# Hybrid attention and RG-LRU layer: x loaded ahead of the modulation weights, an early 64-byte read, and the scaling of x moved behind the first h

## The chip, the cores and the metric

The kernel runs on one core of one Trainium2 chip. A core has TensorE (PE, with its weight loads as PEld), VectorE (DVE), ScalarE (ACT), GpSimd (POOL) and SyncE (SP), which work side by side and wait for each other through semaphores, and 16 DMA engines that serve the transfers issued from SP and ACT. The metric is the device time of one execution in microseconds, as the median of several runs.

## The reference, cut to what matters

The input x is 512 rows of 1024 float32. Everything in the opening serves the modulated, normalised h and its first product:

```python
c_act = jax.nn.silu(c)
mod = c_act @ w_mod[l] + b_mod[l]
shift, scale, gate = jnp.split(mod, 3, axis=-1)
h = rmsnorm(x, norm_gain[l]) * (1.0 + scale[:, None, :]) + shift[:, None, :]
proj = h @ w_in[l]
```

The 3072 columns of proj feed block-sparse causal attention (8 heads of 64, rotary), a gated linear recurrence with a width-4 convolution, and two SiLU gates. Both branches are normalised and gated, go through one output projection, and are added to x with the gate; a last RMSNorm follows.

## The kernel before, in words

All products run on TensorE in a split form: each operand is a high part (rounded to TensorE's fp32r) and a low part (what is left), and three products of parts stand for one float32 product. h is kept transposed, as eight chunks h0 to h7 of 128 channels by 512 rows. The first phase makes h chunk by chunk and multiplies each with the first seven column blocks of w_in (`w0_d`, 896 columns): 21 matmuls of 512 columns a chunk (L406), which accumulate in seven PSUM banks (`acc`). The remaining blocks follow, with attention, recurrence and gates woven in, then the output projection (`po`).

What one chunk d needs:

- **x**: four row tiles x0 to x3 (128 rows by 1024). ACT squares and sums each (L334, `scr`), takes the root (L338, `ss`), DVE takes the reciprocal (L340). Then the tile is scaled by its row factor in place (L344 on ACT or L346 on DVE, columns 128 to 1023). Columns 0 to 127, which chunk 0 needs, are scaled apart into `xs`. TensorE transposes the four tiles' columns of a chunk into a PSUM bank `xp` (L392 for chunk 0, L388 for the others).
- **g**: two columns, gain and shift of the chunk. DVE multiplies the chunk's modulation weights (`ws`, from the array `wss`, one row of shift and one of scale for each channel) by the broadcast SiLU of c (`cb`) and sums along the row (L368 for chunk 0, in four halves of 512; L372 for the rest, two of 1024). Three small operations make g of the sums (L376, L377, L380).
- **h**: ACT applies g to `xp` twice (L395), once rounded (`h0h`), once not; DVE's subtraction (L397) gives the low part `h0l`.
- **w0**: ACT rounds the weights (L231, `w00512h` and `w00384h` in chunk 0), DVE subtracts (L249, `w00512l`).

All transfers of the opening are issued by SP in program order on one queue. Until h0 is there, TensorE is given 42 matmuls on a constant tile (`warm`, L306), whose result nobody reads.

The order of the instructions is set at build time by a planner (`Plan.emit`): every `op` has an engine, an estimated cost, the buffers that it reads and writes, an earliest start (`after`) and a due time. The planner walks through an estimated time and gives each engine the ready operation with the earliest due time; an operation with a second way (`alt`) may go to either engine. Changing a due time or a cost can so reorder engines far behind the place of the edit. Each engine then runs its list strictly in that order.

Of the kernel before, what the change touches and what calls it, by code (L numbers as in the profile page):

```python
# [10 lines left out]
AF = mybir.ActivationFunctionType  # L11
OP = mybir.AluOpType
# [3 lines left out]
D = 1024  # L16
# [3 lines left out]
BIG = 3.0e38  # L20
LRU_C = 8.0
NFIRST = 7
NWARM = 42
MOVE = 3.4

V_GAIN, V_SHIFT, V_SCALE, V_GATE = 0, 8, 16, 24
# [33 lines left out]
class Plan:  # L60
# [11 lines left out]
    def op(self, eng, cost, fn, r=(), w=(), due=None, table=None, lat=0.25, after=0.0, alt=None):  # L72
        o = Op(eng, cost, fn, list(r), list(w), due, table, lat, after, alt)
        deps = set()
        for b in o.r:
            if b.writer is not None:
                deps.add(b.writer)
        for b in o.w:
            if b.writer is not None:
                deps.add(b.writer)  # L80
            deps.update(b.readers)
        for b in o.r:
            b.readers.append(o)
        for b in o.w:
            b.writer, b.readers = o, []
        for b in set(o.r) | set(o.w):
            b.users += 1
        deps.discard(o)
        o.deps = list(deps)
        for d in deps:  # L90
            d.outs.append(o)
        o.left = len(deps)
        self.ops.append(o)
        return o
# [82 lines left out]
def tile_hymba_block(ctx: ExitStack, tc: tile.TileContext, x, wss, wgt, win0, wv, winr,  # L177
                     wo, wg, vecs, fgain, consts, out):
    nc = tc.nc
    V, A, G, PE, SP = nc.vector, nc.scalar, nc.gpsimd, nc.tensor, nc.sync  # L180
# [18 lines left out]
    op = plan.op  # L199
# [4 lines left out]
    def t4(name, dt=F32, shape=(128, 1024)):  # L204
        return Buf("t4", list(shape), dt, name)

    def bank(name, kind=None):
        return Buf("ps", [128, 512], F32, name, kind)

    def col(name):  # L210
        return Buf("c", [128, 2], F32, name)

    def fix(name, shape, dt=F32):
        return Buf("fix", list(shape), dt, name)


    def dv(n, ptr=0):
        return 0.075 + n / 960.0 + 0.06 * ptr

    def dv2(n, ptr=0):  # L220
        return 0.14 + n / 1920.0 + 0.06 * ptr

    def ac(n, ptr=0, acc=0):
        return 0.09 + n / 1200.0 + 0.1 * ptr + 0.1 * acc

    def acp(n, ptr=0, acc=0):
        return ac(n, ptr, acc) - 0.039
# [6 lines left out]
    def pe(n, passes=1):  # L234
        return passes * n / 2250.0

    def load(dst, src, due, kb=512, queue=SP):
        op("SP", kb / 390.0, lambda: queue.dma_start(dst[:], src), [], [dst], due, lat=1.1 if due < T_REST - 8 else 3.3)  # L238
# [17 lines left out]
    def like(t):  # L256
        return lambda name, dt: t4(name, dt, t.shape)


    def t_first(d):  # L260
        return T_FIRST + 4.79 * d

    T_FIRST, T_REST, STEP = 12.3, 50.7, 0.94

    def t_step(n):
        return T_REST + STEP * n
# [3 lines left out]

    xt = [t4(f"x{t}") for t in range(NT)]
    vec, ident, cst = fix("vec", [128, NV]), fix("ident", [128, 128]), fix("cst", [128, 2048])
    load(vec, vecs, -100, kb=40)
    for t in range(NT):
        load(xt[t], x[t * 128:(t + 1) * 128, :], -99 + 0.5 * t)
    ws, w0 = {}, {}
    for d in range(ND):
        if d == 0:
# [25 lines left out]
    op("V", 0.3, lambda: V.memset(warm[:], 1.0), [], [warm], -10)  # L304
    for n in range(NWARM):
        op("PE", 0.32 if n < 11 else 0.235, lambda: PE.matmul(spare[:], warm[:, 0:128], warm[:], start=True, stop=True),  # L306
# [9 lines left out]
    cb = t4("cb")  # L316
# [10 lines left out]


    xs = [Buf("t2", [128, 128], F32, f"xs{t}") for t in range(NT)]
    xdue = (5.0, 6.3, 7.6, 8.9)  # L330
    scr = [t4("scr0"), t4("scr1")]
    for t in range(NT):
        ss, due = col("ss"), xdue[t]
        op("A", ac(1024, 0, 1), lambda t=t, ss=ss: A.activation(  # L334
            scr[t % 2][:], xt[t][:], AF.Square, accum_out=ss[:, 0:1]), [xt[t]], [scr[t % 2], ss], due,
           alt=("V", dv(1024), lambda t=t, ss=ss: V.scalar_tensor_tensor(
               scr[t % 2][:], xt[t][:], 1.0, xt[t][:], op0=OP.mult, op1=OP.mult, accum_out=ss[:, 0:1])) if t == 9 else None)
        op("A", 0.2, lambda ss=ss: A.activation(ss[:, 1:2], ss[:, 0:1], AF.Sqrt, bias=epsc[:, 0:1], scale=1.0 / D),  # L338
           [ss, epsc], [ss], due + 0.2, "sqrt")
        op("V", 0.1, lambda ss=ss: V.reciprocal(ss[:, 0:1], ss[:, 1:2]), [ss], [ss], due + 0.3)  # L340
        for dst, cut, late in ((xs[t], slice(0, 128), 0.4), (xt[t], slice(128, D), 2.5)):
            o = (lambda d_, c_: d_[:] if d_ in xs else d_[:, c_])
            n = cut.stop - cut.start
            op("A", ac(n, 1), lambda t=t, ss=ss, dst=dst, cut=cut, o=o: A.activation(  # L344
                o(dst, cut), xt[t][:, cut], AF.Copy, scale=ss[:, 0:1]), [ss, xt[t]], [dst], due + late,
               alt=("V", dv2(n, 1), lambda t=t, ss=ss, dst=dst, cut=cut, o=o: V.tensor_scalar(  # L346
                   o(dst, cut), xt[t][:, cut], ss[:, 0:1], None, op0=OP.mult)))


    h = [t2(f"h{d}") for d in range(ND)]  # L350
# [4 lines left out]
                                         op0=OP.add), [vec], [vec], -3)  # L355

    sch = col("sch")

    def part(d, j):
        return ws[d][j][:, j] if d >= 4 else ws[d][j][:]  # L360

    def gain(d):

        sc, g = col("sc"), col("g")
        for j in (1, 0):
            if d == 0:
                for n in range(2):
                    op("V", dv(512), lambda j=j, n=n: V.scalar_tensor_tensor(  # L368
                        ws[0][j][n][:], ws[0][j][n][:], 1.0, cb[:, 512 * n:512 * n + 512], op0=OP.mult, op1=OP.mult,
                        accum_out=(sch if n else sc)[:, j:j + 1]), [ws[0][j][n], cb], [ws[0][j][n], sch if n else sc], 7 + n)  # L370
                continue
            op("V", dv(1024), lambda j=j: V.scalar_tensor_tensor(  # L372
                part(d, j), part(d, j), 1.0, cb[:], op0=OP.mult, op1=OP.mult, accum_out=sc[:, j:j + 1]),
               [ws[d][j], cb], [ws[d][j], sc])
        if d == 0:
            op("V", 0.1, lambda: V.tensor_add(sc[:], sc[:], sch[:]), [sc, sch], [sc], 10)  # L376
        op("V", 0.2, lambda: V.tensor_scalar(  # L377
            g[:, 1:2], sc[:, 1:2], vec[:, V_SCALE + d:V_SCALE + d + 1], vec[:, V_GAIN + d:V_GAIN + d + 1],
            op0=OP.add, op1=OP.mult), [sc, vec], [g])
        op("V", 0.1, lambda: V.tensor_add(g[:, 0:1], sc[:, 0:1], vec[:, V_SHIFT + d:V_SHIFT + d + 1]), [sc, vec], [g])  # L380
        return g

    for d in range(ND):
        g, xp = gain(d), bank(f"xp{d}")

        def turn(xp=xp, d=d):
            for t in range(NT):
                PE.transpose(xp[:, t * 128:(t + 1) * 128], xt[t][:, d * 128:(d + 1) * 128], ident[:])  # L388
        if d:
            op("PE", 0.44, turn, xt + [ident], [xp], t_first(d) - 3.8)  # L390
        for t in range(NT if not d else 0):
            op("PE", 0.11, lambda t=t, xp=xp: PE.transpose(xp[:, t * 128:(t + 1) * 128], xs[t][:], ident[:]),  # L392
               [xs[t], ident], [xp], 7 + 0.5 * t)
        for o in (hh[d], h[d]):
            op("A", acp(512, 2), lambda o=o, d=d, xp=xp, g=g: A.activation(  # L395
                o[:], xp[:], AF.Identity, bias=g[:, 0:1], scale=g[:, 1:2]), [xp, g], [o])
        op("V", dv(512), lambda d=d: V.tensor_sub(hl[d][:], h[d][:], hh[d][:].bitcast(F32)), [h[d], hh[d]], [hl[d]])  # L397
        if d:
            wp = [split(w0[d], like(w0[d]), f"w0{d}", 128 * NFIRST)] * 2
        else:  # L400
            wp = [split(w, lambda name, dt, w=w: Buf("t2", w.shape, dt, name), w.name, w.shape[1], late=[g]) for w in w0[0]]
        for i, (a, b) in enumerate(((0, hh[d]), (1, hh[d]), (0, hl[d]))):
            for j in range(NFIRST):
                w, k = wp[j // 4][a], j if d else j % 4
                op("PE", pe(512), lambda w=w, k=k, b=b, j=j, first=(d == 0 and i == 0), last=(d == ND - 1 and i == 2):
                   PE.matmul(acc[j][:], w[:, k * 128:(k + 1) * 128], b[:], start=first, stop=last),  # L406
                   [w, b], [acc[j]], t_first(d) + (0.62 if d else 1.6) * i + 0.21 * j)
# [329 lines left out]
    for g in range(4):  # L737
        br, half = "la"[g // 2], g % 2
# [11 lines left out]
        for t in range(NT):  # L750
            m = slice(t * 128, (t + 1) * 128)
            cuts = (0, 256, 512) if g == 3 and t == NT - 1 else (0, 512)
            for n, (lo, up) in enumerate(zip(cuts, cuts[1:])):
# [15 lines left out]
                o, q = t2("o"), half + n  # L769
                if w < 512:  # L770
                    op("V", dv(w, 1), lambda t=t, c0=c0, c1=c1, o=o, q=q: V.scalar_tensor_tensor(
                        o[:, :c1 - c0], res[t][:, c0:c1], 1.0, res[t][:, c0:c1], op0=OP.mult, op1=OP.mult,
                        accum_out=ssq[t][:, q:q + 1]), [res[t]], [ssq[t], o], t1 + 0.2)
# [107 lines left out]
```

## Time and profile before

| What | Value |
|---|---|
| Median of 3 runs | 243.88 us (243.81 to 247.26) |
| The profiled execution's own time | 243.72 us |
| Its span, first to last instruction | 242.0 us |
| PE busy | 232.3 us (96%) |
| DVE busy | 196.2 us (81%) |
| ACT busy | 144.3 us (60%) |
| Mean granted TensorE clock | 0.994 |

The profile and the trace are of one execution. Times inside it are counted from the start of its span; the 1.72 us between span and execution time lie outside of all instructions. Busy times of consecutive instructions overlap by their pipelines, so a matmul of 0.39 us can follow the one before after 0.23 us; where a sum is made, the distance from start to start counts.

### The profile page before, as it was taken

How to read it: one execution, taken by the hardware profiler on the slowest of the kernel's cores; microseconds unless marked ns; L12 is line 12 of the kernel's file. 1: busy time of each engine (PE TensorE's matmuls, PEld its weight loads, DVE VectorE, ACT ScalarE, POOL GpSimd, SP SyncE). 2: the span in 40 equal slices, each digit the busy share in tenths (PEclk: the TensorE clock that was granted, in tenths of full speed). 3: DMA queues.
4: the chain of work that ended last, by engine and by line, in shares of the span. 5: the costliest groups of instructions: out<-in, count | busy, mean ns of one | idle time of the engine just before them, and what ended most of it. 6: DMA issues, size and time to landing. Idle time of an engine off the chain costs nothing.

```text
span 242.0 us, 3301 instructions
## 1 busy us (share of the span) xinstructions
PE 232.3 (96%) x1134; PEld 184.5 (76%) x1134; DVE 196.2 (81%) x364; ACT 144.3 (60%) x264; POOL 12.0 (5%) x32
## 2 busy tenths in 40 slices
PE   7899999999999989999999999999999999999990
PEld 4357888888888868788888688886888868888880
DVE  3499989979745899996799999999999999326473
ACT  7685373675224296439899999695664934003362
POOL 1000000018800000000000000000000000000000
PEclk9999999999999999999999999999999999999997
DMA  6999999922799877045079997292221300000045
GB/s 211 311 408 409 419 417 412 368 91 57 171 270 230 209 282 227 37 173 173 0 178 297 208 270 265 77 364 83 88 88 39 134 3 0 0 0 0 3 160 186
DMA packets 15087, 44.29 MB, mean 183 GB/s; under 512 B 2144, under 2 KB 2784, under 8 KB 14432
## 3 DMA queue, kind: packets, MB, share of 16 engines
q1 hardware_dynamic: 14928, 43.96, 54.9%
q8 instruction: 9, 0.15, 0.3%
q10 hardware_dynamic: 144, 0.13, 0.2%
q14 instruction: 6, 0.05, 0.1%
HBM read 35.69 MB, written 2.10 MB: 156 GB/s over the span
## 4 chain that ended last, share of the span: by engine, by line
PE 78%; DMA 9%; ACT 4%; SPq 3%; DVE 2%; issue 1%; ACTq 0%
PE acc L406 16%; PE pj L241 10%; PE pj L243 9%; PE pj L242 9%; PE po L241 6%; PE po L243 6%; PE po L242 6%; DMA wc<-in_winr_dram 6%; PE av L582 4%; PE sc L559 4%; DMA x<-in_x_dram 3%; PE tp L603 3%; SPq L465 2%; ACT x L344 1%; SPq L238 1%; PE xp L388 1%
## 5 line engine op out<-in xcount | busy, mean ns | idle before, releaser
L570 ACT ACTIVATE z<-z,mn 128x128 f32<-128x128 f32 (+3 forms) x32 | 17.8, 557 | 10.8 <-DVE mn L567 10.6
L567 DVE CUSTOM_DVE_ANT_0 z<-sc,cst 128x128 f32<-128x128 f32 (+3 forms) x32 | 14.6, 485 | 6.2 <-PE sc L559 6.2
L372 DVE SCALAR_TENSOR_TENSOR ws<-ws,cb 128x1024 f32<-128x1024 f32 x14 | 16.8, 1219 | 0.0
L231 ACT COPY pt<-tp 128x128 f32<-128x128 f32 (+3 forms) x29 | 10.7, 415 | 9.4 <-PE tp L603 9.2
L306 PE MATMUL spare<-warm 128*128 128x512 bf16 x42 | 12.4, 435 | 1.5 <-DVE warm L304 1.5
L603 PE MATMUL tp<-ident,z 128*128 128x128 f32 x80 | 12.1, 273 | 0.6 <-ACT z L570 0.6
L603 PEld LDWEIGHTS tp<-ident,z 128*128 128x128 f32 x80 | 9.8, 140 | 3.6 <-ACT z L570 1.3
L775 ACT ACTIVATE o<-xr 128x512 f32<-128x512 f32 x7 | 4.4, 633 | 11.8 <-DVE xr L764 11.8
L764 DVE SCALAR_TENSOR_TENSOR xr<-po,rba,xr 128x512 f32<-128x512 f32 (+1 forms) x9 | 6.2, 691 | 6.3 <-PE po L243 6.2
L764 DVE SCALAR_TENSOR_TENSOR xr<-po,rbl,xr 128x512 f32<-128x512 f32 x8 | 6.0, 748 | 6.0 <-PE po L243 6.0
L530 DVE SCALAR_TENSOR_TENSOR wgt<-wgt,cb 128x1024 f32<-128x1024 f32 x8 | 9.8, 1219 | 0.0
L306 PEld LDWEIGHTS <-warm 128*128 128x128 bf16 x42 | 4.7, 113 | 6.6 <-issue 2.5
L747 DVE TENSOR_TENSOR wo<-wo,grow 128x1024 f32<-128x1024 f32 x8 | 9.7, 1214 | 0.0
L582 PE MATMUL av<-pt,v 128*64 128x512 f32 (+3 forms) x64 | 9.5, 439 | 0.0
L484 DVE SCALAR_TENSOR_TENSOR xc<-xl,vec,xc 128x511 f32<-128x511 f32 (+2 forms) x12 | 8.9, 743 | 0.1
L582 PEld LDWEIGHTS av<-pt,v 128*64 128x64 f32 x64 | 4.2, 136 | 5.2 <-issue 4.2
L625 ACT ACTIVATE sz<-pj 128x512 f32<-128x512 f32 x8 | 4.8, 597 | 3.7 <-PE pj L243 3.7
L729 ACT ACTIVATE rba<-ss,epsc 128x4 f32<-128x4 f32 x1 | 0.3, 263 | 10.2 <-PE ss L727 10.2
L626 DVE SCALAR_TENSOR_TENSOR sz<-sz,pj 128x512 f32<-128x512 f32 x8 | 5.5, 682 | 0.9 <-ACT sz L625 0.9
L395 ACT ACTIVATE h<-xp,g 128x512 f32<-128x512 f32 x8 | 6.2, 770 | 0.0
L570 ACT ACTIVATION_READ_ACCUMULATOR z<-z,mn 128x1 f32 x32 | 6.0, 188 | 0.0
L334 ACT ACTIVATE scr<-x 128x1024 f32<-128x1024 f32 x4 | 4.2, 1057 | 2.9 <-DMA x<-in_x_dram 2.9
(1119 smaller groups left out, 771.0 us busy)
## 6 DMA issues: line engine op xcount, KB each, us to landing
wc<-in_winr_dram SPq DMA_DIRECT2D x13, 512.0 KB, 5.4
ws<-in_wss_dram SPq DMA_DIRECT2D x4, 1024.0 KB, 12.8
wgt<-in_wgt_dram SPq DMA_DIRECT2D x8, 512.0 KB, 4.0
wo<-in_wo_dram SPq DMA_DIRECT2D x8, 512.0 KB, 4.1
w<-in_win_dram SPq DMA_DIRECT2D x7, 448.0 KB, 8.6
ws<-in_wss_dram SPq DMA_DIRECT2D x6, 512.0 KB, 7.9
x<-in_x_dram SPq DMA_DIRECT2D x4, 512.0 KB, 5.1
wv<-in_wv_dram SPq DMA_DIRECT2D x4, 512.0 KB, 7.6
```

The source lines that it names most:

```text
L231: op("A", acp(n) if psum else ac(n), lambda: A.copy(dst(), src()), r, w, due, after=after, alt=("V", dv(n) if psum else dv2(n), lambda: V. ...
L241: PE.matmul(ps, lh, rh, start=start, stop=False)
L242: PE.matmul(ps, lh, rl, start=False, stop=False)
L243: PE.matmul(ps, ll, rh, start=False, stop=stop)
L306: op("PE", 0.32 if n < 11 else 0.235, lambda: PE.matmul(spare[:], warm[:, 0:128], warm[:], start=True, stop=True), [warm], [spare], 5.3 + ...
L372: op("V", dv(1024), lambda j=j: V.scalar_tensor_tensor(part(d, j), part(d, j), 1.0, cb[:], op0=OP.mult, op1=OP.mult, accum_out=sc[:, j:j + ...
L406: PE.matmul(acc[j][:], w[:, k * 128:(k + 1) * 128], b[:], start=first, stop=last),
L567: op("V", dv(n) + 0.085, lambda s=s, z=z: V.tensor_tensor_reduce(out=z[:, :n], in0=ps[s][:, :n], in1=cst[:, 2048 - n:2048], op0=OP.add, op ...
L570: op("A", ac(n, 1, 1), lambda s=s, z=z: A.activation(z[:, :n], z[:, :n], AF.Exp, bias=mn[s][:, 0:1], scale=-1.0, accum_out=sm[:, i, s:s + ...
L582: PE.matmul(ps2[64 * s:64 * s + 64, k * 128:], vt[k][:, (2 * p + s) * 64:(2 * p + s + 1) * 64], pts[s][:, k, k * 128:], start=(k == 0), st ...
L603: PE.transpose(tp[:, k * 128:(k + 1) * 128], z[:, k * 128:(k + 1) * 128], ident[:])
L764: op("V", dv(w, 1), lambda t=t, ps=ps, c0=c0, c1=c1, br=br: V.scalar_tensor_tensor(res[t][:, c0:c1], ps[:, :c1 - c0], rb[br][:, t:t + 1], ...
```

## The change

It edits the opening. SP issues all four tiles of x before the modulation weights. ACT issues, as its first instruction, a transfer of 16 columns of the weights of chunk 0 (64 bytes on each of 128 rows) into a tile `touch` that nobody reads. The engines of the scaling are fixed: `xs0` and `xs1` on DVE, `xs2` and `xs3` and all four large scalings on ACT; those of x1, x2 and x3 are kept until after h0 by an earliest start (`REST`). The gain of chunk 0 is made of half sums with b_mod added in between, so that one small operation instead of three stands behind the last sum. The transposes of chunk 1 are due 2.2 us later, the constant matmuls are 31 instead of 42, and two base times of the planner are 0.5 us earlier.

```diff
-NWARM = 42
+NWARM = 31
+REST = (0.0, 12.9, 13.0, 13.1)
...
-    T_FIRST, T_REST, STEP = 12.3, 50.7, 0.94
+    T_FIRST, T_REST, STEP = 11.8, 50.2, 0.94
...
+    touch = fix("touch", [128, 16])
+    op("A", 0.1, lambda: A.dma_start(touch[:], wss[0][:, 0, 0:16]), [], [touch], -100)
     load(vec, vecs, -100, kb=40)
     for t in range(NT):
-        load(xt[t], x[t * 128:(t + 1) * 128, :], -99 + 0.5 * t)
+        load(xt[t], x[t * 128:(t + 1) * 128, :], -99 + 0.3 * t)
...
-    xdue = (5.0, 6.3, 7.6, 8.9)
+    xdue = (4.0, 5.0, 6.0, 7.0)
...
-        for dst, cut, late in ((xs[t], slice(0, 128), 0.4), (xt[t], slice(128, D), 2.5)):
+        for dst, cut, e, due2, after in ((xs[t], slice(0, 128), "VVAA"[t], due + 0.4, 0.0), (xt[t], slice(128, D), "A", 20.0 + t, REST[t])):
             o = (lambda d_, c_: d_[:] if d_ in xs else d_[:, c_])
             n = cut.stop - cut.start
-            op("A", ac(n, 1), lambda t=t, ss=ss, dst=dst, cut=cut, o=o: A.activation(
-                o(dst, cut), xt[t][:, cut], AF.Copy, scale=ss[:, 0:1]), [ss, xt[t]], [dst], due + late,
-               alt=("V", dv2(n, 1), lambda t=t, ss=ss, dst=dst, cut=cut, o=o: V.tensor_scalar(
-                   o(dst, cut), xt[t][:, cut], ss[:, 0:1], None, op0=OP.mult)))
+            if e == "A":
+                op("A", ac(n, 1), lambda t=t, ss=ss, dst=dst, cut=cut, o=o: A.activation(
+                    o(dst, cut), xt[t][:, cut], AF.Copy, scale=ss[:, 0:1]), [ss, xt[t]], [dst], due2, after=after)
+            else:
+                op("V", dv2(n, 1), lambda t=t, ss=ss, dst=dst, cut=cut, o=o: V.tensor_scalar(
+                    o(dst, cut), xt[t][:, cut], ss[:, 0:1], None, op0=OP.mult), [ss, xt[t]], [dst], due2, after=after)
...
+        half = (sc, sch)
         for j in (1, 0):
             if d == 0:
                 for n in range(2):
...
-                        accum_out=(sch if n else sc)[:, j:j + 1]), [ws[0][j][n], cb], [ws[0][j][n], sch if n else sc], 7 + n)
+                        accum_out=half[n][:, j:j + 1]), [ws[0][j][n], cb], [ws[0][j][n], half[n]], 8 - 2 * j + 0.7 * n)
+                    if not n:
+                        op("V", 0.1, lambda j=j, v=(V_SHIFT, V_SCALE)[j]: V.tensor_add(
+                            sc[:, j:j + 1], sc[:, j:j + 1], vec[:, v:v + 1]), [sc, vec], [sc], 9.2)
+                if j:
+                    op("V", 0.2, lambda: V.tensor_scalar(g[:, 1:2], sch[:, 1:2], sc[:, 1:2], vec[:, V_GAIN:V_GAIN + 1],
+                                                         op0=OP.add, op1=OP.mult), [sc, sch, vec], [g], 9.4)
+                else:
+                    op("V", 0.1, lambda: V.tensor_add(g[:, 0:1], sch[:, 0:1], sc[:, 0:1]), [sc, sch], [g], 9.5)
                 continue
...
         if d == 0:
-            op("V", 0.1, lambda: V.tensor_add(sc[:], sc[:], sch[:]), [sc, sch], [sc], 10)
+            return g
...
-            op("PE", 0.44, turn, xt + [ident], [xp], t_first(d) - 3.8)
+            op("PE", 0.44, turn, xt + [ident], [xp], t_first(d) - (3.8 if d > 1 else 1.6))
```

What that does to the order of the instructions is seen at three places. In the names, the number behind the underscore is a build number: x_90, x_99, x_116 and x_133 are the row tiles x0 to x3 before, x_92, x_101, x_118 and x_131 after, and ws_129 or ws_142 is the first half row of modulation weights.

SP's queue at the start, first before, then changed:

```order
L238 DMA x_116<-in_x_dram 128x1024
L238 DMA ws_129<-in_wss_dram 128x512
L238 DMA x_133<-in_x_dram 128x1024
L238 DMA ws_148<-in_wss_dram 128x512
L238 DMA ws_158<-in_wss_dram 128x512
```

```order
L239 DMA x_118<-in_x_dram 128x1024
L239 DMA x_131<-in_x_dram 128x1024
L239 DMA ws_142<-in_wss_dram 128x512
L239 DMA ws_148<-in_wss_dram 128x512
L239 DMA ws_159<-in_wss_dram 128x512
```

The fourth tile of x and the first half row of weights have changed places; all that follows on the queue is in the old order up to the fifties of microseconds.

ACT between the last squares and h, before and changed:

```order
L334 ACTIVATE scr_125,ss<-x_133 128x1024
L338 ACTIVATE ss<-ss,epsc 128x1
L344 ACTIVATE x_99<-x_99,ss 128x896
L344 ACTIVATE x_116<-x_116,ss 128x896
L231 CAST w00512h<-w_176 128x512
L344 ACTIVATE x_133<-x_133,ss 128x896
L395 ACTIVATE h0h<-xp_150,g 128x512
L395 ACTIVATE h_233<-xp_150,g 128x512
L231 CAST w01h<-w_1_224 128x896
L395 ACTIVATE h1h<-xp_226,g 128x512
```

```order
L337 ACTIVATE scr_127,ss<-x_131 128x1024
L341 ACTIVATE ss<-ss,epsc 128x1 x2
L348 ACTIVATE x_92<-x_92,ss 128x896
L348 ACTIVATE xs_190<-x_118,ss 128x128
L348 ACTIVATE xs_197<-x_131,ss 128x128
L232 CAST w00512h<-w_178 128x512
L232 CAST w00384h<-w_185 128x384
L409 ACTIVATE h0h<-xp_150,g 128x512
L409 ACTIVATE h_218<-xp_150,g 128x512
L348 ACTIVATE x_101<-x_101,ss 128x896
L348 ACTIVATE x_118<-x_118,ss 128x896
L348 ACTIVATE x_131<-x_131,ss 128x896
```

Ahead of `h0h`, three large scalings have become one, and two small ones and one more rounding have come in. The other three large ones stand between the second h of chunk 0 and `h1h`, and the rounding of `w01` has gone to DVE. On DVE the same stretch now reads:

```order
L374 SCALAR_TENSOR_TENSOR ws_142,sc<-ws_142,cb 128x512
L374 SCALAR_TENSOR_TENSOR ws_148,sch<-ws_148,cb 128x512
L343 RECIPROCAL ss<-ss 128x1 x2
L378 TENSOR_TENSOR sc<-sc,vec 128x1
L381 TENSOR_SCALAR g<-sch,sc,vec 128x1
L374 SCALAR_TENSOR_TENSOR ws_159,sc<-ws_159,cb 128x512
L374 SCALAR_TENSOR_TENSOR ws_167,sch<-ws_167,cb 128x512
L378 TENSOR_TENSOR sc<-sc,vec 128x1
L384 TENSOR_TENSOR g<-sch,sc 128x1
L250 TENSOR_TENSOR w00512l<-w_178,w00512h 128x512
L250 TENSOR_TENSOR w00384l<-w_185,w00384h 128x384
```

The four weighted sums stand close together; the two reciprocals that ACT's small scalings wait for are behind the second of them.

TensorE around the first matmuls with h, before and changed:

```order
L388 MATMUL xp_226<-ident,x_90 128x128
L388 MATMUL xp_226<-ident,x_99 128x128
L388 MATMUL xp_226<-ident,x_116 128x128
L388 MATMUL xp_226<-ident,x_133 128x128
L306 LDWEIGHTS warm
L306 MATMUL spare<-warm 128x512
L406 MATMUL acc_236<-h0h,w00512h 128x512
```

```order
L420 MATMUL acc_241<-h0h,w00384l 128x512
L420 MATMUL acc_222<-h0l,w00512h 128x512
L402 MATMUL xp_260<-ident,x_92 128x128
L402 MATMUL xp_260<-ident,x_101 128x128
L402 MATMUL xp_260<-ident,x_118 128x128
L402 MATMUL xp_260<-ident,x_131 128x128
L420 MATMUL acc_226<-h0l,w00512h 128x512
```

The transposes of chunk 1 stood ahead of chunk 0's first matmul and now stand behind its fifteenth. Eight constant matmuls stood between the transposes of `xs3` and those of chunk 1; now one stands behind `xs3`, and the two that stood within chunk 0's 21 matmuls are gone.

## Rows read from the trace of the kernel before

**Rows 1.** page, part 1: busy us, share of the span, instructions, by engine

```profile
PE 232.3 (96%) x1134; PEld 184.5 (76%) x1134; DVE 196.2 (81%) x364; ACT 144.3 (60%) x264; POOL 12.0 (5%) x32
```

**Rows 2.** chain of waits to 30 us: start us, us, engine, what, line

```profile
3.11 8.01 DMA x<-in_x_dram
...
11.14 1.16 ACT scr L334 x2
...
12.62 1.86 ACT x L344 x2
...
14.90 1.04 ACT x L344
15.94 0.68 ACT h0h L395
...
16.65 2.60 PE acc L406 x10
...
24.30 4.82 PE acc L406 x21
```

**Rows 3.** all waits of TensorE: who waited for whom, us, times, longest

```profile
PE spare L306 <- DVE warm L304: 1.5, 1, 1.5
PE xp L392 <- DVE xs L346: 1.1, 1, 1.1
PE tp L603 <- ACT z L570: 0.6, 1, 0.6
```

**Rows 4.** by stretches: PE, PEld, DVE, ACT, POOL busy; PEclk, DMA share, GB/s

```profile
4.00:5.00 1.00, 1.00 (x7) 1.00 (x6) 0.26 (x1) 0.50 (x3) 0.00 (x0) 1.00 1.01 397
7.00:9.00 2.00, 2.00 (x11) 1.03 (x10) 0.45 (x2) 1.60 (x6) 0.00 (x0) 1.00 0.97 157
12.00:13.00 1.00, 1.00 (x7) 0.49 (x5) 1.00 (x3) 0.97 (x4) 0.00 (x0) 1.00 1.04 396
```

**Rows 5.** ACT in order of time: start us, us, operation, idle before and releaser

```profile
4.77 1.06 ACT L334 ACTIVATE scr<-x 128x1024 f32<-128x1024 f32 x1 [0.49 <-DMA x<-in_x_dram]
...
6.17 1.06 ACT L334 ACTIVATE scr<-x 128x1024 f32<-128x1024 f32 x1 [0.25 <-DMA x<-in_x_dram]
...
7.91 1.06 ACT L334 ACTIVATE scr<-x 128x1024 f32<-128x1024 f32 x1 [0.40 <-DMA x<-in_x_dram]
...
8.96 0.47 ACT L338 ACTIVATE ss<-ss,epsc 128x1 f32<-128x1 f32 x2
...
14.39 0.60 ACT L231 CAST w00512h<-w 128x512 fp32r<-128x512 f32 x1
```

**Rows 6.** DVE in order of time, the same columns, around the sums

```profile
9.71 0.69 DVE L368 SCALAR_TENSOR_TENSOR ws<-ws,cb 128x512 f32<-128x512 f32 x1 [1.69 <-DMA ws<-in_wss_dram]
...
10.33 0.68 DVE L346 TENSOR_SCALAR x<-x,ss 128x896 f32<-128x896 f32 x1
...
11.82 0.69 DVE L368 SCALAR_TENSOR_TENSOR ws<-ws,cb 128x512 f32<-128x512 f32 x1
...
14.24 0.16 DVE L376 TENSOR_TENSOR sc<-sc,sch 128x2 f32<-128x2 f32 x1
...
16.94 1.23 DVE L372 SCALAR_TENSOR_TENSOR ws<-ws,cb 128x1024 f32<-128x1024 f32 x1
...
18.56 0.69 DVE L397 TENSOR_TENSOR h0l<-h,h0h 128x512 fp32r<-128x512 f32 x1
```

**Rows 7.** PEld in order of time: the constant matmuls' weight loads

```profile
5.78 0.15 PEld L306 LDWEIGHTS <-warm 128*128 128x128 bf16 x1 [0.28 <-issue]
6.21 0.15 PEld L306 LDWEIGHTS <-warm 128*128 128x128 bf16 x1 [0.28 <-issue]
...
7.06 1.22 PEld L306 LDWEIGHTS <-warm 128*128 128x128 bf16 x6 [0.28 <-issue]
```

**Rows 8.** groups by line and shape: xcount, busy us, mean ns of one

```profile
L231 ACT COPY pt<-tp 128x128 f32<-128x128 f32 x8 | 1.7, 265 | 3.3 <-PE tp L603 3.3
```

**Rows 9.** DMA issues of 5.2 to 5.5 us: KB, us to landing

```profile
w<-in_win_dram SPq DMA_DIRECT2D x1, 256.0 KB, 8.6
```

## The prediction, made before the changed kernel ran

> **What bounds the kernel now.** Read the busy shares first: TensorE is busy for 232.3 of 242.0 us [rows 1]. Its waits say the same more sharply: it waited three times in all, 1.5 us at the very start, 1.1 us for a scaled tile of x before h, and 0.6 us once in the middle [rows 3]. So the end of the kernel is set by when real matmuls begin, and by nothing that adds a wait behind that. The chain of waits then shows what sets the beginning [rows 2]: a transfer of x until 11.1, ACT's square and root of the last tile, large scalings of x at 12.62 and 14.90, h0h at 15.94, and the first matmul with h at 16.65. From there the chain is TensorE alone, 21 matmuls in 4.82 us, 0.23 each. The reader should see two costs in it: the last tile of x is late, and ACT does three large scalings that chunk 0 doesn't need before it makes h0h.
>
> Why is x late? ACT began the squares of x0, x1 and x2 when they landed, at 4.77, 6.17 and 7.91 [rows 5]; the fourth came only at 11.14. Half a row tile of weights was in between, which at 396 GB/s is 0.66 us. The rest is a hole: from 7 to 9 us the 16 DMA engines were as occupied as ever (share 0.97) but moved 157 GB/s instead of 397 [rows 4], so 480 KB are missing, or 1.2 us. Check: 7.91 + 1.40 (one tile, from x0 to x1) + 0.66 + 1.2 = 11.17. The hole falls on the first transfer that reads the modulation weights, the one that DVE waited for until 9.71 [rows 6]; the rate is back at 396 later, when the same array and w_in are read.
>
> **The change, part by part.** *x first.* The fourth tile should land at 7.91 + 1.40 = 9.31 in place of 11.14.
>
> *The early read.* No row shows one. Its cost lies between nothing (64 bytes a row, while the queues start up) and the whole hole of 1.2 us moved in front of x; its gain between nothing and the hole. I take that the hole goes: the slow stretch goes with a first access, and the first access is then made while vec and x start. The weights' halves then land at 9.97, 10.63, 11.3 and 11.95, and w0 of chunk 0, issued at about 5.3 and landed 8.6 later [rows 9], at about 12.6 and 13.1. ACT issues it ahead of its first work; x0 finds ACT idle for 0.49 us [rows 5], which covers an issue.
>
> *ACT to h0h.* Square 1.16 [rows 2] to 10.47; two roots 0.47 [rows 5] to 10.94; one large scaling, 0.93 (half of 1.86 [rows 2]), to 11.87; two 128-wide scalings at 0.27 each, by the 128-wide copy [rows 8], to 12.4; the 512-wide rounding when its weights land, 12.6, from start to next start 0.51 [rows 2, 5], to 13.1; the 384-wide one between 0.27 and 0.60, taken as 0.45, to 13.55.
>
> *DVE to g.* Four sums of 0.69, two reciprocals and four small operations of about 0.2 [rows 6]: 9.97 + 1.38 = 11.35, + 0.8 = 12.15, + 1.38 = 13.53, + 0.4 = 13.93. So DVE is the later by 0.4, and h0h starts at 13.95. Its 0.76 and the hand-over were 0.8 from ACT's start to the first matmul (0.68 and 0.71 after the overlap, by the chain [rows 2]): the first matmul at **14.75, 1.9 us earlier**.
>
> *Behind h0h.* Three large scalings, 0.93 each, stand after the second h, so the last tile is ready at 13.95 + 2 x 0.68 + 3 x 0.93 = 18.1. TensorE asks for it after fifteen matmuls: ten in 2.60 and five of 0.23 [rows 2] give 18.5. Not late, by 0.4. The low part h0l is closer: DVE does two subtractions (0.69, and 0.52 for 384 columns), two sums of 1.23 and h0l, 0.69 [rows 6], so 13.93 + 4.36 = 18.3; TensorE asks for it after fourteen matmuls, at 18.27. Then chunk 1: g needs 0.4 and one rounding of 896 columns, which is new on DVE (0.68, as x0's scaling [rows 6]), so h1h starts at 19.4 and feeds a matmul at 20.2; TensorE is through its four transposes and six matmuls at 18.5 + 0.44 + 1.38 = 20.3. Margins of 0 to 0.4 us, so I charge 0.2.
>
> *Work that changes on TensorE.* Chunk 1's transposes, 0.44, come into the stream; two constant matmuls, 0.46, leave it. Nothing.
>
> *Downstream.* DVE, ACT and TensorE are ordered a little differently from some 50 us on, because the planner starts from other times. I charge nothing: TensorE's real matmuls keep their order to the eighth column block, and its one wait there is 0.6.
>
> The sum against the profiled execution: 243.72 - 1.9 + 0.2 = 242.0. The median of the runs is 0.16 above that execution, so **242.1 us**, 0.7% faster.
>
> **A rule that bears on it.** The hole shows the DMA engines occupied and slow at once [rows 4]: what waits there waits on an engine, not in the queue. The Trainium skill ("DMA: Bandwidth & Descriptors", section "Issuing engines are not separate DMA queues") says that transfers issued from ACT and from SP end up on the same 16 engines and interleave. By that rule the slow first accesses of the early read are interleaved with x0 and hold it up; the sum would be that of the next paragraph, and no row here shows two queues at work in the opening.
>
> **The rivals.** *The hole stays, with the weights or in front of x.* Either way the weights land as before: x3 now ahead of them, the first half at 11.17, the second at 11.84. DVE goes 11.17 + 1.38 + 0.8 + 1.38 + 0.4 = 15.13, the first matmul at 15.95, a gain of 0.7 in place of 1.9, with the same 0.2 behind it: 243.88 - 0.5 = 243.4. For it: a slow first access has to be paid somewhere, and if the engines stand still for it, x pays. Against it: the read is issued before any tile of x is under way.
>
> *The clock falls (the slower side).* Before, TensorE had something to do until 16.65, its longest pause being 1.1 us, and the matmuls kept their pace. Eleven constant matmuls are taken out, those closest to h0. After the transposes of the last small tile, at 12.4, one is left: TensorE stands idle from about 12.7 to 14.75, 2.0 us. If that is enough, the first h matmuls run at the low level. At the start of the trace the constant matmuls follow at 0.43 us, 1.2 GHz for 512 columns, until 7.06, and at 0.20 to 0.23 then, the 2.4 GHz level [rows 7] (the granted clock reads 1.00 in all of these rows, so the spacing has to be read). That was 5.5 us from the first matmul at 1.5 [rows 3]. Another 5.5 us at 0.43 hold 12.8 matmuls that would take 2.95 us: a loss of 2.55, and 242.1 + 2.55 = 244.7, slower than before. It decides from a pause somewhere above the 1.1 us seen to be harmless. The Trainium skill ("TensorE: Matmul & The Clock Gate", section "Why this matters for your kernels") asks for no long pauses between bursts of matmuls, since the array then falls back to half its clock. Whether 2 us are long, no row here shows.
>
> *A new wait downstream.* DVE and ACT have other orders in the attention and gates; one more wait like the one seen costs 0.6 [rows 3], two 1.2: 242.7 to 243.3. For it: DVE is busy 81% of the whole span [rows 1]. Against it: TensorE waited once in all that time.
>
> **How the numbers follow.** The forecast has 0.47; the hole that stays 0.28; a new wait 0.13; the clock 0.09; 0.03 is left for more gain than I count, where roots, scalings and sums overlap better (241.0 and less). The predicted time is that of the likeliest, 242.1. The range reaches from 241.0, where ACT's and DVE's steps are all at the lower bounds, to 243.7, the hole that stays with a further 0.3 of waiting in chunks 0 and 1; it leaves out the clock case and the last 0.03. All of these lie within 2% of 243.88 (239.0 to 248.8), and 2% is about what a measurement of this kernel tells from no change: within 0.97, faster 0.01, slower 0.02, the last for a clock that falls and several new waits together.
>
> **What would show it.** In the profile after: the four squares of x without a pause, the last at about 9.3; no stretch before 14 us in which the DMA share is near 1 and the rate far below 390 GB/s; h0h at about 14 with DVE's g just before it; the first acc matmul at 14.75; a list of TensorE's waits with one of about 2 us before it and small ones in chunk 0 and 1; a spacing of 0.23 right after the pause. If the rate falls before x0 has landed, or again around 10 us, the hole stayed. If the spacing is 0.43 behind the pause, the clock fell. If the first matmul is 1.9 us earlier and the end is not, look for a new wait between 60 and 200 us: that would make the step "downstream: nothing" the wrong one.

## Result: 0.5% faster, within what counts as no change, and the profile after

The changed kernel ran in 242.79 us (median of 20 runs, 241.07 to 245.41) against 243.88 for the kernel before (20 runs); the ratio is 0.9946, interval 0.9926 to 0.9966. The ratios here and below leave out the executions more than 1.5% above the fastest of their kernel, three of these 20; the medians hold them. Forecast were 242.1 and "within 2%". A second series of 12 runs, the experiment *again* below, gave 243.18 and 0.9953 [0.9923, 0.9984]. What strikes is the spread: the executions of one kernel lie 4 us apart, and the fastest are 1.7 us better than the median. The profiled execution took 243.68 us, almost as long as the profiled one before.

TensorE's busy time (page, part 1; us, share, instructions) fell from 232.3 [rows 1], by its eleven constant matmuls fewer, and the span didn't follow (241.9, from 242.0):

```profile
PE 229.6 (95%) x1123; PEld 183.0 (76%) x1123; DVE 198.4 (82%) x367; ACT 142.5 (59%) x262; POOL 11.6 (5%) x32
```

So it stands still for longer. Read first where it starts with h. The chain of waits of the changed kernel (start us, us, what, line) answers to [rows 2]:

```profile
5.33 8.50 DMA w<-in_win_dram
...
13.85 0.62 ACT w00512h L232
...
14.79 0.78 ACT h0h L409
...
15.61 3.71 PE acc L420 x15
19.32 0.44 PE xp L402 x4
```

The first matmul with h stands at 15.61 in place of 16.65: 1.04 us earlier, not the 1.9 forecast. The chain no longer goes through x and its scalings; it goes through the transfer of chunk 0's w, which lands at 13.83. Why that is late, the stretches show (as in [rows 4]; us, PE, PEld, DVE, ACT and POOL busy, clock, DMA share, GB/s):

```profile
7.00:8.00 1.00, 1.00 (x6) 0.46 (x5) 0.04 (x1) 0.93 (x3) 0.00 (x0) 1.00 1.01 401
8.00:9.00 1.00, 1.00 (x6) 0.45 (x5) 0.41 (x2) 0.81 (x1) 0.00 (x0) 1.00 1.06 281
9.00:10.00 1.00, 0.91 (x5) 0.20 (x2) 0.41 (x2) 1.00 (x4) 0.00 (x0) 1.00 0.90 137
10.00:11.00 1.00, 0.90 (x5) 0.53 (x6) 0.26 (x2) 1.00 (x5) 0.00 (x0) 1.00 1.04 350
```

Engines occupied, 281 and 137 GB/s: the hole has stayed, behind x now. Against 400 GB/s, 8 to 11 us lack 119 + 263 + 50 = 432 KB, 1.1 us. ACT in order of time (as in [rows 5]) shows that x itself came first as meant, and where ACT then waited:

```profile
4.84 1.06 ACT L337 ACTIVATE scr<-x 128x1024 f32<-128x1024 f32 x1 [0.43 <-DMA x<-in_x_dram]
...
9.46 1.06 ACT L337 ACTIVATE scr<-x 128x1024 f32<-128x1024 f32 x1
...
12.60 0.69 ACT L348 ACTIVATE xs<-x,ss 128x128 f32<-128x128 f32 x2 [0.69 <-DVE ss L343]
13.85 0.62 ACT L232 CAST w00512h<-w 128x512 fp32r<-128x512 f32 x1 [0.56 <-DMA w<-in_win_dram]
...
16.13 2.90 ACT L348 ACTIVATE x<-x,ss 128x896 f32<-128x896 f32 x3
19.80 0.78 ACT L409 ACTIVATE h1h<-xp,g 128x512 fp32r<-128x512 f32 x1 [0.77 <-PE xp L402]
```

DVE's sums (as in [rows 6]) waited for the same weights, and g was complete at 14.32 + 0.16 = 14.48, 0.3 before h0h started:

```profile
10.79 0.69 DVE L374 SCALAR_TENSOR_TENSOR ws<-ws,cb 128x512 f32<-128x512 f32 x1 [0.74 <-DMA ws<-in_wss_dram]
...
11.79 0.69 DVE L374 SCALAR_TENSOR_TENSOR ws<-ws,cb 128x512 f32<-128x512 f32 x1 [0.31 <-DMA ws<-in_wss_dram]
...
14.32 0.16 DVE L384 TENSOR_TENSOR g<-sch,sc 128x1 f32<-128x1 f32 x1
```

Then read where this execution lost its 1.04 us again. TensorE's waits (who for whom: us, times, longest), against [rows 3]:

```profile
PE acc L420 <- ACT h0h L409: 1.7, 1, 1.7
PE tp L617 <- ACT z L584: 1.6, 1, 1.6
PE spare L309 <- DVE warm L307: 1.5, 1, 1.5
PE xp L406 <- ACT xs L348: 0.9, 1, 0.9
PE xp L406 <- DVE xs L351: 0.2, 1, 0.2
```

The wait for z, a product of the attention, near 86 us, was 0.6 and is 1.6. So it gave back 1.0. ACT stands there in front of a rounding of the combining weights, wc2h, whose transfer (wc) is late, although both z had been ready for it since 82.97 + 0.08 us:

```profile
84.26 1.05 ACT L232 CAST wc2h<-wc 128x1024 fp32r<-128x1024 f32 x1 [5.45 <-DMA wc<-in_winr_dram]
85.22 0.81 ACT L494 ACTIVATE xc<-xl,vec 128x512 f32<-128x512 f32 x1
85.93 0.60 ACT L584 ACTIVATE z<-z,mn 128x384 f32<-128x384 f32 x1
```

DVE's side of it:

```profile
82.97 0.08 DVE L581 DVE_READ_ACCUMULATOR2_ANT mn<- 128x1 f32 x1
```

### The profile page after: what moved, and what is told of

It reads as the page before. It is cut to its first block, busy times and chain, and to the rows that moved or that the text cites. A ratio compares the mean times of both kernels' runs of the same rounds, so it can differ in the third digit from the quotient of the medians.

```text
span 241.9 us, 3282 instructions
## 1 busy us (share of the span) xinstructions
PE 229.6 (95%) x1123; PEld 183.0 (76%) x1123; DVE 198.4 (82%) x367; ACT 142.5 (59%) x262; POOL 11.6 (5%) x32
## 4 chain that ended last, share of the span: by engine, by line
PE 78%; DMA 9%; SPq 4%; DVE 3%; ACT 2%; issue 1%; ACTq 0%
PE acc L420 16%; PE pj L242 10%; PE pj L244 9%; PE pj L243 9%; PE po L242 6%; PE po L244 6%; PE po L243 6%; PE av L596 4%; PE sc L573 4%; DMA w<-in_win_dram 4%; PE tp L617 3%; DMA wc<-in_winr_dram 3%; DMA k1hs<-k0h 3%; SPq L239 2%; SPq L479 2%; PE xp L402 1%
## 5 line engine op out<-in xcount | busy, mean ns | idle before, releaser
L232 ACT COPY pt<-tp 128x128 f32<-128x128 f32 (+3 forms) x28 | 10.0, 408 | 11.1 <-PE tp L617 11.0
L309 PE MATMUL spare<-warm 128*128 128x512 bf16 x31 | 9.4, 448 | 1.5 <-DVE warm L307 1.5
L309 PEld LDWEIGHTS <-warm 128*128 128x128 bf16 x31 | 3.6, 118 | 5.1 <-issue 1.8
L232 ACT COPY rc<-rs 128x512 f32<-128x512 f32 x3 | 1.8, 587 | 6.6 <-PE rs L606 6.6
```

Of the source, the lines that this page charges most:

```text
L232: op("A", acp(n) if psum else ac(n), lambda: A.copy(dst(), src()), r, w, due, after=after, alt=("V", dv(n) if psum else dv2(n), lambda: V. ...
```

## The experiments

The planner's order is kept fixed in these kernels: the list that it chose for the changed kernel (`chosen`, in order of issue over all engines) is edited before the instructions are emitted. `at(engine, buffer, k)` finds the k-th operation of an engine that writes a buffer, `move(i, j)` puts operation i where j stands. So nothing shifts but what is named.

**again**: the changed kernel as it is.

> The changed kernel unaltered, as the yardstick of this group. Expected 0.992 to 0.997 of before (about 242.6 to 243.0 us where before gives 243.9). In its trace the first matmul with h at 15.6 us again and the slow DMA stretch near 9 us again. One theory: the 1.6 us for which TensorE waits at about 86 us belongs to this program (ACT's order holds it up), so it is there again, between 1 and 2 us. Rival: it was a mishap of one execution, and is 0.6 us or less here.

243.18 us (241.27 to 245.32). Its profiled execution took 241.27, 2.4 less than the first. The first h matmul was at 15.23, and wc2h at 81.90, so that z caused no wait:

```profile
15.23 3.71 PE acc L420 x15
...
81.90 1.05 ACT L232 CAST wc2h<-wc 128x1024 fp32r<-128x1024 f32 x1 [3.73 <-DMA wc<-in_winr_dram]
```

From 78 to 82 us all transfers together ran at 333 GB/s here and at 241 in the first execution, with a DMA share of 1.01 and 1.00. The wait at 86 us is thus a matter of the execution.

**no_touch**: the early read alone taken out.

```
+ chosen.pop(at("A", "touch"))
```

> The changed kernel without the early read; every other instruction in the same order. Theory: the early read does nothing, since its own packets were not slow and the slow stretch of 1.2 us still falls on the first half row of modulation weights; the time is that of the changed kernel within 0.3 us and the first matmul with h at 15.5 to 15.7. Rival: the read removes part of the stretch; without it the first matmul is 0.3 to 1.2 us later and the time longer by as much.

243.28 us (241.66 to 248.96), ratio 0.997 [0.994, 1.0001]. The first h matmul came at 15.10, no later than with the read; 8 to 10 us ran at 195 and 156 GB/s. The read did nothing against the hole. But the 15 matmuls that follow took 5.29 us in place of 3.71:

```profile
15.10 5.29 PE acc L432 x15
```

The granted clock was 0.50 there from 16 to 19 us.

**x3_late**: the last tile of x back behind the first half row of weights.

```
+ move(at("SP", "x3"), at("SP", "ws010"))
```

> The changed kernel with the fourth tile of x behind the first half row of weights again, as before; all else in the changed order. Theory: x3 lands at about 11.1 instead of 9.4, its square, the roots, x0's scaling, two small scalings and two roundings then put h0h at 15.2 instead of 14.8, so 0.4 us slower than the changed kernel: a minor part of the gain. Rival: x first is most of the gain, and the kernel loses 1.0 us, back to before.

243.81 us, 0.9956 [0.9919, 0.9994]; first h matmul at 15.52, the hole one microsecond earlier. h0h started at 14.70, not at the 15.2 expected. Fetching x whole first is worth nothing that shows.

**mid**: the rounding wc2h behind the two z.

```
+ move(at("A", "wc2h"), at("A", "z", 5))
```

> The changed kernel with one instruction moved: ACT rounds the column block wc2 behind the two 384-wide exponentials instead of ahead of them. Theory: the wait of 1.6 us of TensorE at 86 us is ACT standing in front of wc2's transfer with z ready 3 us before; the wait goes, 0.5 to 1.6 us faster than the changed kernel, about 241.5 us. Rival: TensorE waits as long one step later, for wc2 itself or for v; then the same time as the changed kernel.

243.13 us (242.37 to 245.15), 0.9973 [0.9947, 0.9999]. The wait for z went, as expected; but in this execution the clock fell. The stretches of *mid*:

```profile
14.00:15.00 1.00, 0.00 (x0) 0.00 (x0) 0.70 (x4) 1.00 (x3) 0.00 (x0) 1.00 1.02 414
15.00:16.00 1.00, 0.35 (x1) 0.36 (x2) 1.00 (x3) 1.00 (x2) 0.00 (x0) 0.87 1.03 411
16.00:17.00 1.00, 1.00 (x3) 0.75 (x3) 0.95 (x3) 1.00 (x2) 0.00 (x0) 0.50 1.03 411
17.00:18.00 1.00, 1.00 (x4) 0.79 (x3) 1.00 (x1) 1.00 (x2) 0.00 (x0) 0.50 1.02 407
18.00:19.00 1.00, 1.00 (x4) 0.81 (x3) 1.00 (x5) 1.00 (x2) 0.00 (x0) 0.50 1.02 410
19.00:20.00 1.00, 1.00 (x5) 0.77 (x5) 1.00 (x3) 0.06 (x1) 0.00 (x0) 0.92 1.03 407
```

and one of the changed kernel in its first execution, then the h matmuls of *mid* in its chain:

```profile
16.00:17.00 1.00, 1.00 (x6) 0.82 (x5) 0.94 (x3) 1.00 (x2) 0.00 (x0) 1.00 1.03 409
```

```profile
15.65 5.30 PE acc L434 x15
```

TensorE is fully busy in both, but gets three or four matmuls into the microsecond at 0.50 (1.2 GHz) and six at 1.00 (2.4 GHz). 15 matmuls in 5.30 us, not 3.71: 1.6 us lost. So two things that come and go could make the spread: the clock and the wait for z. The next four kernels, run together, part them.

**fill**: the pauses before h filled with constant matmuls.

```
+ w = chosen[at("PE", "spare")]
+ for k in range(7): chosen.insert(at("PE", "acc0"), w)
+ for k in range(3): chosen.insert(at("PE", "xp0", 2), w)
```

> The changed kernel with seven more constant matmuls on TensorE straight ahead of the first h matmul and three ahead of the transposes of the third small tile of x, so that the pause of 1.7 to 1.9 us before the first h matmul is filled; nothing else moves. Theory (in some executions the granted clock falls in that pause, and 15 h matmuls then take 5.3 us in place of 3.7): no fall in the profile, the 15 matmuls in 3.7 us, the first h matmul at 15.2 to 15.8, and a median of 241.8 to 242.4 with a narrower spread than the changed kernel's 241.1 to 245.4. Rival 1 (the spread has another cause, downstream): the clock stays up and the median is that of the changed kernel, 242.8 to 243.2. Rival 2 (constant matmuls in front of h delay it): first h matmul 0.3 to 1 us later, median 243.2 to 244.

242.36 us, 0.9942 [0.9912, 0.9972]. First h matmul at 15.45, the 15 matmuls in 3.72 (a line of its chain), and one short pause left before it (a line of its waits):

```profile
15.45 3.72 PE acc L436 x15
```

```profile
PE xp L422 <- ACT xs L364: 0.6, 1, 0.6
```

The spread fell to 2.5 us and the runs split: seven of 12 runs at 241.3 to 242.4, five at 243.4 to 243.9, none between.

**fill_mid**: the same, and the edit of *mid*.

> The same filled pause, and ACT's rounding of the third half of the combining weights (wc2h, which waits for its transfer at 84 us) moved behind the two 384-wide products z that TensorE waits for there. Theory (two causes make up the spread, the clock in the pause and this wait of up to 1.6 us): no fall, no wait of TensorE at 84 to 87 us above 0.3, median 241.2 to 242.0, below both kernels. Rival 1 (the wait at 86 us is only a symptom of late transfers and comes back elsewhere): as the kernel with the filled pause alone, within 0.3. Rival 2 (neither matters): 242.8 to 243.2.

241.60 us, 0.9916 [0.9882, 0.995]; ten of 12 runs at 241.1 to 242.0. The upper group shrank from five runs to two, as it would if the wait for z made it. Twelve runs of each don't prove that, and no run of the upper group has a trace: of the wait for z it is shown that it costs 0 to 1.6 us in one execution or another, not how much of the spread it makes.

**fill_scale_ahead**: *fill* with the three large scalings back ahead of chunk 0's rounding.

```
+ for t in (1, 2, 3): move(at("A", f"x{t}"), at("A", "w00512h"))
```

> The filled pause, and the three large scalings of x1 to x3 put back ahead of ACT's rounding of chunk 0's weights, as far as ACT's order allows; they are the part of the change that speaks of fewer steps before the scale of h. Theory (ACT's chain to h0h is what the change shortened): three times 0.93 us of which ACT's idle time of 0.6 to 1.2 us hides some, so the first h matmul 1.6 to 2.4 us later than with the filled pause alone, 17.0 to 18.0, and the time 1.3 to 2.3 us longer. Rival (the weights' late landing sets h0h, and ACT's scalings are hidden beside it): first matmul less than 0.7 us later and the time within 0.6.

245.41 us, 1.006 [1.0027, 1.0093], 3.05 above *fill*; between the fastest runs of both it is 243.58 - 241.33 = 2.25. Its chain:

```profile
13.14 1.23 ACT x L368 x2
...
14.91 1.02 ACT x L368
15.94 0.51 ACT w00512h L252
16.45 0.41 ACT w00384h L252
16.86 0.69 ACT h0h L429
...
17.59 3.71 PE acc L440 x15
```

The first h matmul is 2.14 us later than in *fill* and 0.94 later than in the kernel before: without this part of the change, three scalings behind the first h, nothing is gained. It isn't the kernel before again. There one of the four large scalings was DVE's [rows 6], here ACT does all four ahead of h0h, so 2.14 is more than this part can have gained. Seven of ten runs lie 1.6 us and more above the fastest; the pause before h0h is 2.3 us here, and a fall of the clock would cost that much. The one trace, of the fastest run, shows none, but the mean granted clock (below, behind *gap*) is low in six of the ten runs. The median of the other four is 244.0, 1.7 above *fill*.

**gap**: the last ten constant matmuls of the changed kernel left out.

```
+ for k in range(10): chosen.pop([i for i, o in enumerate(chosen) if o.w[0:1] and o.w[0].name == "spare"][-1])
```

> The changed kernel without the last ten constant matmuls, so that TensorE's pause ahead of the first h matmul grows by about 2.2 us. Theory (the pause is at the edge, and sometimes the clock falls): here it falls in every profile, 15 h matmuls take 5.3 us in place of 3.7, and the median is 0.8 to 1.6 us above the changed kernel's, 243.6 to 244.6. Rival 1 (the clock falls for another reason than the pause): the median is that of the changed kernel, 242.8 to 243.2. Rival 2 (a longer pause costs more than a short one): 245 and more.

244.65 us, 1.004 [1.001, 1.0069], and never under 244.09. The clock was 0.79 at 15 to 16 us, 0.50 until 18, 0.51 to 19; the 15 matmuls took 5.21 us. Its waits:

```profile
PE xp L419 <- ACT xs L361: 2.7, 1, 2.7
PE acc L433 <- ACT h0h L422: 1.8, 1, 1.8
...
PE xp L419 <- DVE xs L364: 0.9, 1, 0.9
```

The pause ahead of h0h is as long as it was; the one that grew, to 2.7, stands ahead of the transposes of the small tiles. In this trace a longer pause does not cost more (5.21 us for the 15 matmuls); it makes the loss the rule. Without these ten matmuls the changed kernel is 0.4% slower than the one before: the fall costs more than the opening gains.

How often the clock falls can be read from all runs, since each has its mean granted clock on record. The five traces in which it fell at h (*no_touch*, *mid*, *gap*, and *touch_j1* and *w0_first* below) have 0.984 to 0.990, the nine others 0.991 to 0.997. The two groups almost touch, so a single run near the border can be misread. Of the 32 runs of the changed kernel (the first series and *again*) 13 have 0.990 or less, with a median of 243.74 against 242.26 for the other 19: 1.5 us, close to the 1.6 of the traces. Of *fill*, *fill_mid* and *fill_mid_nt* (below) not one of 34 runs is so low, of *gap* all ten are. So filling the pauses keeps the clock up, and the upper group of *fill* is not the clock's. The kernel before has 0.990 or less in 14 of its 98 runs beside the experiments, all of them at 245.3 us or above.

The last four asked about the hole, and put together what had helped. **touch_j1**: the early read from the half that is transferred first.

```
- A.dma_start(touch[:], wss[0][:, 0, 0:16])
+ A.dma_start(touch[:], wss[0][:, 1, 0:16])
```

> The changed kernel with its early read of 64 bytes a row taken from the half of the modulation weights that is transferred first (j=1); the changed kernel reads them from the other half (j=0). Theory (the slow stretch comes when the large packets begin, and an early read of any 64 bytes does not take it away): the stretch stays, two slices between 8 and 11 us under 300 GB/s and some 430 to 480 KB missing, first h matmul 15.1 to 15.7. Rival (a first access to that very region is slow, and the change touched the wrong half): no slice under 380 GB/s from 6 to 12 us, the first half row lands 1.1 us earlier, and the first h matmul at 14.4 to 14.8.

One run, 244.15 us. 8 to 10 us at 283 and 135 GB/s, first h matmul at 15.25: reading the right half early doesn't help either. (The clock fell, 15 matmuls in 5.31.)

**w0_first**: chunk 0's w ahead of the modulation weights.

```
+ move(at("SP", "w00512"), at("SP", "ws010"))
+ move(at("SP", "w00384"), at("SP", "ws010"))
```

> The changed kernel with the 512-wide and the 384-wide transfer of chunk 0's w (from another array) issued ahead of the modulation weights' four half rows. Theory A (the first bulk read of each array is slow): a slow stretch at w's transfers from 8 to 9 us and a second one of like size at the modulation weights, more than 800 KB missing in all. Theory B (it comes once, at a place in time or at the first packets that are not x's): about 430 to 480 KB missing in all, at w's transfers alone, and the modulation weights at 84 ns a 2-KB packet. Theory C (it belongs to the modulation weights alone): w at full rate until some 10.2 us, then a slow stretch of 430 to 480 KB.

One run, 245.59 us, with the clock fallen. Stretches (us, clock, DMA share, GB/s):

```profile
8.00:9.00 1.00, 1.00 0.99 390
9.00:10.00 1.00, 1.00 1.13 328
10.00:11.00 1.00, 1.00 0.81 124
11.00:12.00 1.00, 1.00 0.84 297
```

Theory C: w, in 2-KB rows too, runs at 390; the hole comes with the modulation weights, once, 451 KB of it (72 + 276 + 103).

**fill_mid_nt**: *fill_mid* without the early read.

> The filled pause, the rounding wc2h behind the two products z, and no early read: the version that the experiments point to. Theory: as with the early read, within 0.3 us of 241.6, most executions between 241.1 and 242.0, no fall of the clock, no wait at 84 to 87 us; faster than the kernel before by 0.6 to 1.1%. Rival (the early read is worth something): 0.4 us and more above, and the first h matmul after 15.6.

241.60 us, 0.9914 [0.9885, 0.9943], the median of *fill_mid* to the hundredth. No fall, TensorE's waits 0.5 and 0.3 behind the start. This is the best version: 1.2 to 1.6 us under the changed kernel's two medians, though these are from other series and the intervals of the ratios overlap.

**ws_first**: *fill_mid_nt* with the first half row of modulation weights ahead of x.

```
+ move(at("SP", "ws010"), at("SP", "x0"))
```

> The best version so far (pause filled, rounding wc2h behind z, no early read) with the first half row of the modulation weights, 256 KB, transferred ahead of x0. Theory (the slow stretch goes with the first bulk transfer of the modulation weights, wherever it stands): it moves to the front, no slice under 380 GB/s from 8 to 12 us, but x lands later. If the slow 1.1 us are hidden in the start-up of the queues before 6 us, the last tile of x lands at 9.8 to 10.1, the 512-wide weights at 12.0 to 12.4 and the first h matmul comes at 14.2 to 14.8, 0.3 to 0.9 earlier than without the move, median 240.7 to 241.4. Rival 1 (the stretch is paid in full in front of x): the last tile of x lands at 10.6 to 11.2, first h matmul 15.4 to 16.0, median 241.8 to 242.6. Rival 2 (it belongs to a later part of the weights too): another stretch under 300 GB/s between 8 and 12 us.

244.93 us, 1.004 [1.0002, 1.0079]. The hole moved to the front and later stretches are clean:

```profile
3.00:4.00 1.00, 1.00 0.76 86
4.00:5.00 1.00, 1.00 0.72 131
5.00:6.00 1.00, 1.00 0.92 260
...
9.00:10.00 1.00, 1.00 1.05 424
```

Without the move 3 to 6 us ran at 356, 401 and 373, so 653 KB are missing, more than before. All three sums were too low: the first square moved to 8.32 us, the other three followed it without a gap, and the first h matmul came at 17.66, 2.6 later; 0.8 of that because h0h (done at 16.84) found constant matmuls queued ahead of it:

```profile
17.66 3.45 PE acc L441 x15
```

It is the mechanism of rival 1, at a higher price. The clock has a part in the median: it was up in the trace, but six of the ten runs have a mean of 0.990 or less; the median of the other four is 243.7.

## Why the prediction was right in kind, and which steps failed

*The early read* failed. I took the hole for a first access that 64 bytes a row could make in advance. It stays with the early read, without it, and with the read from the right half; it goes where the first bulk transfer of the modulation weights goes (*w0_first*, *ws_first*). Whether the read held up x, the runs don't settle: the first square stands at 4.50 in *no_touch*, against 4.84 and 5.08 in the changed kernel's two traces, but at 4.76 in *fill_mid_nt* and 4.77 in the kernel before [rows 5], both without the read, and at 4.73 in *mid*, with it. The Trainium skill ("DMA: Bandwidth & Descriptors", section "Issuing engines are not separate DMA queues") has ACT's transfers share the 16 engines with SP's. These traces neither bear that out nor speak against it.

*x first* was right as told (fourth square at 9.46, x landed before) and without an effect that shows, since w, not x, now comes last (*x3_late*).

*ACT to h0h* and *DVE to g* went by the rival of the hole that stays: first matmul forecast at 15.95 there, measured at 15.61 and 15.23. That rival had DVE as the later one; ACT was, 14.79 against 14.48, because it waited 0.56 for w. By first matmuls the change gains 1.0 to 1.4, not 1.9; that it gains comes from the scalings, as forecast (*fill_scale_ahead*: with all four ahead of h0h the first matmul is later than before).

*Behind h0h* was charged 0.2 and cost nothing: fifteen matmuls, chunk 1's transposes and the next matmuls follow each other without a pause, the last scaling ending at 19.03, 0.3 before TensorE asks for it.

*The clock* was a rival with 0.09, priced at 2.55. With the changed kernel's own stock of constant matmuls and order of transfers ahead of h, or nearly so, it came in three of six traces (the first five rows of the table), and by the mean clock in 13 of the 32 runs of the changed kernel itself. It costs 1.6: in *mid* the low level lasted 0.26 + 3 + 0.16 = 3.4 us, not the 5.5 that I took from the start of the trace. Pauses of TensorE between 7.5 us and the first h matmul, by the lists of waits:

| kernel | pauses, us | 15 h matmuls, us |
|---|---|---|
| changed; again | 0.9 + 0.2 + 1.7; 0.8 + 1.7 | 3.71; 3.71 |
| x3_late | 1.6 + 1.0 | 3.71 |
| no_touch | 0.6 + 0.6 + 1.8 | 5.29 |
| mid | 1.3 + 1.9 | 5.30 |
| touch_j1 | 1.0 + 0.7 + 1.6 | 5.31 |
| w0_first | 2.2 + 0.5 + 1.5 | 5.18 |
| gap | 2.7 + 0.9 + 1.8 | 5.21 |
| fill, fill_mid, fill_mid_nt | 0.6; 0.6; 0.5 | 3.72 to 3.74 |
| fill_scale_ahead | 0.6 + 2.3 | 3.71 |
| ws_first | 3.1 | 3.45 |

I had asked whether one pause of 2 us is long enough. The rows answer otherwise: the clock fell with 1.5 us before h0h and held with 1.7 and 2.3 there, and with 3.1 in one piece in *ws_first*, behind which 25 constant matmuls stood. Of the other kernels those with the larger sum of pauses lost it; with one trace of most kernels, and the runs of the changed kernel and of *fill_scale_ahead* on both sides, that is an order in a table and not a rule. The Trainium skill ("TensorE: Matmul & The Clock Gate", section "Why this matters for your kernels") warns of long pauses between bursts. The traces agree that pauses can cost the clock, at 1.6 us a time, but not that the length of one pause decides: in *mid* none was over 1.9.

*Downstream: nothing* was wrong for single executions: the wait for z is 0, 0.5, 0.8 or 1.6 us, by when wc lands. The kernel before has it too (0.6 [rows 3]), so it did not come with the change, but it decided what the first profile showed.

The balance: 243.88 x 0.0054 = 1.3 us were gained [0.8 to 1.8], 1.8 were forecast (the prediction's own sum, 243.72 - 1.9 + 0.2 + 0.16, is 242.18 and not 242.1, which changes nothing here). The hole takes 0.5 to 0.9 from the forecast, and the margin of 0.2 that was not spent gives some back. The clock takes 13/32 x 1.6 = 0.65 on average, and the kernel before loses some of the same, 14/98 x 1.6 = 0.2 if a fall costs as much there. That leaves 0.65 to 1.05 (1.8 - 0.9 + 0.2 - 0.65 + 0.2 and 1.8 - 0.5 + 0.2 - 0.65 + 0.2), which the interval holds for the most part, but under the 1.3 measured. How long the wait for z is in the other executions of the kernel before, which has one trace, is not known, so the balance isn't closed to a few tenths.

That the time came out 0.7 us from the forecast is in part luck. The mechanism was right in the scalings, but the hole stayed, which had 0.28 and a sum of 243.4, and the clock fell in a part of the runs, which had 0.09 and a sum of 244.7; a margin that was not needed and the kernel before's own losses covered some of it.

Between the kernel before and *fill_mid* lie 2.0 us (0.84%, 0.50 to 1.18%). That isn't the opening alone: *fill_mid* also has ACT's rounding behind z and no wait there, where the kernel before waited 0.6 [rows 3].

What stays open: why the first bulk read of that array is slow, and what draws the transfers of 66 to 84 us out in some executions.

## What to carry to other kernels

When a change takes filler matmuls out in front of a late start, look at the granted clock of the stretch right behind the start, in more than one execution. A median that moves little with a wide spread is a reason to trace twice and compare TensorE's waits, since causes that come and go can hide what the change does. An operation that waits for a transfer should stand behind those on its engine that are ready and waited for.

## What the runs showed of the hardware that was not expected

The first bulk transfer of one array of several ran for about 2 us at 120 to 300 GB/s instead of 400, with a DMA share between 0.66 and 1.13, at every place behind the first three tiles of x, while x and w did not. It cost 1.0 to 1.35 us (402 KB in *x3_late*, 538 KB in *fill*); ahead of x it cost 1.6 us (653 KB). Early reads of 64 bytes a row did not change that. The granted clock was still 1.00 through most of the pause (*mid*, 14 to 15 us). By slices of 0.2 us it fell within 0.5 us behind the first h matmul in *no_touch*, *mid* and *touch_j1*, and some 0.2 us ahead of it in *gap* and *w0_first*.
